# A float32 transpose: TensorE's start paced by a timed reading on VectorE

## The chip, the core and the metric

The kernel runs on one core of a Trainium2 chip. The metric is the device time of one execution in microseconds, median of three runs. Engines named below: TensorE (PE in the profile, its weight loads PEld), VectorE (DVE), ScalarE (ACT), GpSimd (POOL), SyncE (SP), and the DMA engines that move data between the chip's main memory and SBUF, the on-chip memory.

## The reference

The input x is an array of 8192 x 8192 float32 numbers, 268.4 MB; the output is its transpose:

```python
def reference(x):
    return np.transpose(x)
```

Nothing is computed but the new order. Every byte is read once from main memory and written once.

## The kernel before

**Tiling.** x is cut into T = 128 chunks of 128 rows and 4096 columns (2 MB each): 64 chunks down the left half of the columns, then 64 down the right half. A chunk is loaded by one DMA into `arena` (line 206), each partition holding one row of it. TensorE turns it by 32 transposes of 128 x 128 (line 368) into PSUM, in 16 groups g of two. Group g belongs to lane g of 16: 256 columns of x, which are 256 rows of the output.

**Storing along a diagonal.** Output rows are written in long stretches, so the groups of one lane from 16 successive chunks are collected and stored together, one lane per chunk: store w takes lane w modulo 16. Groups that are not yet due go from PSUM to `slots`; the one that is due in this chunk goes directly to its place in `arena` (line 297 does both). Just before, VectorE's "gather" (line 259) copies the 15 older groups of that lane from `slots` to their place in `arena`. ScalarE copies the first eight groups out of PSUM (half 0), VectorE the last eight (half 1). So the direct copy of chunk t is ScalarE's where t modulo 16 is 0 to 7, and VectorE's where it is 8 to 15. PSUM is full with one chunk: each half is freed for the next chunk when its engine's copies are done (line 305, semaphores s_fra and s_frv). TensorE signals after groups 4, 8, 12 and 16 (semaphore s_pe). Before a chunk's copies, both engines wait for the gather (line 272), since they overwrite what it reads.

**Stores and their space.** A store (line 28) of a full lane is 2 MB in one or two DMAs. The part of `arena` for stores has room for two and a fraction, so the gather for store u waits until store u - 2 has landed (line 247). Loads rotate over three places; the load of chunk t + 3 into the place of chunk t waits until the transposes of t are done. The first chunks are loaded further ahead, and the first and last 15 stores are shorter; the last ones ("flush") follow the last chunk.

**Order.** SyncE issues all loads and stores in one written order on one queue: store t - 1, load t + 2, store t, load t + 3 and so on. The other engines follow semaphores in the order of their own programs.

**TensorE's start.** For chunks E <= t < LAST (12 to 125) TensorE runs a loop over three chunks. Per chunk, in `transposes`: it waits until half 0 is free (line 358), runs IDLE = 4 products of the identity with four copies of itself, 128 x 512, into half 0 of PSUM (line 362, their result is overwritten), waits for the load (line 363), then for the semaphore s_go (line 365), and transposes; half 1 is waited for when group 8 is reached (line 358 again). A product is recorded as two matmuls in the profile. s_go is given by VectorE in `work`: it waits until store u - 2 has landed (line 398) and adds one (line 399), then makes the gather. Chunks before 12 and the last two have neither products nor s_go.

## Time and profile before

| What | Value |
|---|---|
| Median of three runs | 1273.62 us (1271.66 to 1286.72) |
| Profiled execution | 1275.6 us, span 1273.8 us |
| Moved | 537 MB, 422 GB/s on average |
| TensorE, matmuls | 959.7 us busy (75%) |
| TensorE, weight loads | 686.8 us (54%) |
| VectorE | 615.1 us (48%) |
| ScalarE | 257.4 us (20%) |
| Mean granted TensorE clock | 0.961 of full speed |

The span runs from the first to the last instruction of the profiled execution. Busy times include matmuls whose ends are modelled. In rows of the timeline the first number is the start in microseconds, the second the length from the first start to the last end of the merged instructions; in brackets stands how long the engine was idle before, and what released it. In rows of groups the numbers after the bar are the busy time in microseconds and the mean of one in nanoseconds, then the idle time before them. In rows of waits stand the total in microseconds, how many, and the longest. `L368` is line 368; PEq is TensorE's sequencer, whose line tells which wait held it.

### The profile page before, as it was taken

What the parts mean: (1) busy time and instruction counts of PE and PEld (TensorE: products, weight loads), DVE (VectorE), ACT (ScalarE), POOL (GpSimd) and SP (SyncE); (2) the same over time, 40 slices, a digit from 0 to 9 for tenths busy, and PEclk for the clock granted to TensorE, in tenths of its full rate; (3) what the DMA queues carried; (4) which work ended last, traced back from release to release, by engine and by line L of the source; (5) the groups of instructions that cost most, each with busy time, mean ns of one, the idle gap of its engine ahead of it and who ended that gap; (6) DMA issues with size and microseconds to landing.
All of it is one profiled execution on the core that took longest, in us unless ns stands there. A gap on an engine that the chain in (4) does not pass through costs nothing. (4 is left out here: it accounts for less than half of the span.)

```text
span 1273.8 us, 12854 instructions
## 1 busy us (share of the span) xinstructions
PE 959.7 (75%) x5008; PEld 686.8 (54%) x5008; DVE 615.1 (48%) x715; ACT 257.4 (20%) x402; POOL 0.7 (0%) x6
## 2 busy tenths in 40 slices
PE   6669787878777777778778777888877878878730
PEld 6656555555555555555555555655555655555530
DVE  3455455455445544545455444544544445444471
ACT  2222122112211211121112111122111221112210
POOL 0000000000000000000000000000000000000000
PEclk9879999999999999999999999999999899999965
DMA  9999999999999999999999999999999999999997
GB/s 393 411 422 417 427 432 429 431 432 428 432 431 432 432 428 433 431 431 432 428 428 429 431 430 429 424 402 428 396 431 430 422 419 418 425 430 428 417 397 323
DMA packets 41333, 537.09 MB, mean 422 GB/s; under 512 B 4576, under 2 KB 5216, under 8 KB 8288
## 3 DMA queue, kind: packets, MB, share of 16 engines
q1 hardware_dynamic: 41312, 536.89, 99.7%
q14 instruction: 17, 0.14, 0.0%
q8 instruction: 4, 0.07, 0.0%
HBM read 268.44 MB, written 268.44 MB: 421 GB/s over the span
## 5 line engine op out<-in xcount | busy, mean ns | idle before, releaser
L368 PE MATMUL ps<-ident,arena 128*128 128x128 f32 x4096 | 543.4, 293 | 206.2 <-PEq L365 166.8
L368 PEld LDWEIGHTS ps<-ident,arena 128*128 128x128 f32 x4096 | 523.4, 210 | 298.1 <-issue 298.1
L259 DVE COPY arena<-slots 128x2048 f32<-128x2048 f32 (+7 forms) x316 | 304.2, 1012 | 469.8 <-DMA out_dram<-arena 461.5
L362 PE MATMUL ps<-ident 128*128 128x512 f32 x912 | 418.0, 601 | 61.1 <-PEq L358 61.1
L297 ACT COPY slots<-ps 128x1024 f32<-128x1024 f32 (+2 forms) x335 | 238.4, 780 | 488.3 <-DVE arena L259 481.5
L297 DVE COPY slots<-ps 128x512 f32<-128x512 f32 (+2 forms) x336 | 289.4, 913 | 79.6 <-PE ps L368 79.6
L362 PEld LDWEIGHTS ps<-ident 128*128 128x128 f32 x912 | 164.0, 190 | 241.8 <-issue 241.8
L297 ACT COPY arena<-ps 128x256 f32<-128x256 f32 x66 | 24.5, 373 | 478.5 <-DVE arena L259 442.6
L297 DVE COPY arena<-ps 128x256 f32<-128x256 f32 x63 | 26.8, 425 | 87.1 <-PE ps L368 87.0
L297 ACT ACT_TABLE_LOAD x1 | 1.3, 1283 | 1.0 <-SPq L155 1.0
L341 POOL TENSOR_SCALAR_AFFINE_SELECT ident<-ident 128x128 f32<-128x128 f32 x1 | 0.3, 294 | 0.2 <-POOL ident L339 0.2
L339 POOL MEMSET ident<- 128x128 f32 x1 | 0.2, 206 | 0.5 <-SPq L155 0.5
L433 POOL MEMSET const-bfloat16-1.0<- 128x1 bf16 x1 | 0.1, 102 | 0.0
L433 POOL MEMSET const-uint8-127<- 128x1 uint8 x1 | 0.1, 102 | 0.0
L433 POOL MEMSET const-float32-0.0<- 128x1 f32 x1 | 0.1, 99 | 0.2 <-issue 0.2
L433 POOL MEMSET const-float32-1.0<- 128x1 f32 x1 | 0.1, 99 | 0.0
## 6 DMA issues: line engine op xcount, KB each, us to landing
arena<-in_x_dram SPq DMA_DIRECT2D x128, 2048.0 KB, 20.0
out_dram<-arena SPq DMA_DIRECT2D x98, 2048.0 KB, 16.3
out_dram<-arena SPq DMA_DIRECT2D x4, 1920.0 KB, 12.4
out_dram<-arena SPq DMA_DIRECT2D x4, 1792.0 KB, 11.5
out_dram<-arena SPq DMA_DIRECT2D x4, 1664.0 KB, 9.9
out_dram<-arena SPq DMA_DIRECT2D x4, 1536.0 KB, 10.2
out_dram<-arena SPq DMA_DIRECT2D x4, 1408.0 KB, 10.4
out_dram<-arena SPq DMA_DIRECT2D x4, 1280.0 KB, 11.8
```

The source lines that it names most:

```text
L259: cp = nc.vector.tensor_copy(out=ap(arena, do, [[P, len(v)], [dist, B], [1, P]]), in_=ap(slots, so, [[gap, len(v)], [P, B], [1, P]]),)
L297: cp = eng.copy(out=dst, in_=i) if e == 0 else eng.tensor_copy(out=dst, in_=i)
L339: nc.gpsimd.memset(ident, 0.0).then_inc(s_id, 1)
L341: nc.gpsimd.affine_select(out=ident, in_=ident, compare_op=mybir.AluOpType.not_equal, fill=1.0, base=0, pattern=[[-1, P]], channel_multipl ...
L362: nc.tensor.matmul(out=pss[0][:, :4 * P], lhsT=ident, rhs=four, start=True, stop=True)
L368: tr = nc.tensor.transpose(pss[h][:, (u * B + b) * P:(u * B + b + 1) * P], arena[:, q + b:q + PIECE - B + b + 1:B], ident,)
L433: nc = _bacc.Bacc("TRN2", target_bir_lowering=False, num_devices=1)
```

## The change

TensorE starts a chunk's transposes on another signal. VectorE no longer waits for store u - 2 ahead of s_go; it waits for the load of chunk u, takes the maximum over 27 readings of the identity (27 x 128 elements per partition; the result goes to `pad` and is not used), and gives s_go when that is done. The gather follows, with its own waits as before. TensorE now waits for both halves of PSUM at the start of a chunk, runs two products in place of four behind these waits, and waits for s_go ahead of the load's semaphore. All this holds for chunks 6 to 125 in place of 12 to 125.

```diff
-    E = 12
+    E = 6
...
-        nc.alloc_sbuf_tensor("pad", [P, 64], dt)
+        pad = nc.alloc_sbuf_tensor("pad", [P, 64], dt).ap()
...
+        REST = 27
...
-        IDLE = 4
+        IDLE = 2
...
-                if u == 0:
+                if u == 0 and not (h and E <= t < LAST):
                     nc.tensor.sem_inc(s_free[h], -1).wait_op(s_free[h], 1, "sem-ge")
                 if g == 0:
                     if E <= t < LAST:
+                        nc.tensor.sem_inc(s_free[1], -1).wait_op(s_free[1], 1, "sem-ge")
                         for _ in range(IDLE):
                             nc.tensor.matmul(out=pss[0][:, :4 * P], lhsT=ident, rhs=four, start=True, stop=True)
-                    nc.tensor.sem_inc(s_ld[o], -16).wait_op(s_ld[o], 16, "sem-ge")
                     if E <= t < LAST:
                         nc.tensor.sem_inc(s_go, -1).wait_op(s_go, 1, "sem-ge")
+                    nc.tensor.sem_inc(s_ld[o], -16).wait_op(s_ld[o], 16, "sem-ge")
...
                 if E <= u < LAST:
-                    free(nc.vector, ("S", u - 2))
-                    nc.vector.sem_inc(s_go, 1)
+                    nc.vector.wait_ge(s_ld[home["L", u]], 16)
+                    nc.vector.reduce_max(
+                        out=pad[:, :1], in_=ap(ident, 0, [[0, REST], [1, P]]), axis=mybir.AxisListType.XY
+                    ).then_inc(s_go, 1)
                 gather(u, u)
```

## The prediction

> **What bounds the kernel now.** I read the page first, then the waits, then one chunk in order of time.

> ```profile
> span 1273.8 us, 12854 instructions
> q1 hardware_dynamic: 41312, 536.89, 99.7%
> arena<-in_x_dram SPq DMA_DIRECT2D x128, 2048.0 KB, 20.0
> out_dram<-arena SPq DMA_DIRECT2D x98, 2048.0 KB, 16.3
> ```

> The transfers' one queue is busy 99.7% of the span: the DMA engines set the time. A transfer of 2 MB lands 16 to 20 us after its issue, although 2 MB at the 427 GB/s seen below last 4.9 us, so about 10 us of transfers are always queued. An engine may be late by some microseconds without emptying the queue.

> ```profile
> ACT slots L297 <- DVE arena L259: 481.5, 62, 13.6
> DVE arena L259 <- DMA out_dram<-arena: 461.5, 116, 11.4
> ```

> The waits agree: VectorE waits 461.5 us for stores, ScalarE then for VectorE's gather. The timeline shows chunk 65, and what starts chunk 66:

> ```profile
> 607.97 4.08 PE L368 MATMUL ps<-ident,arena 128*128 128x128 f32 x32 [1.48 <-PEq L365]
> 608.02 2.30 DVE L259 COPY arena<-slots 128x2048 f32<-128x2048 f32 x3 [4.17 <-DMA out_dram<-arena]
> ...
> 610.62 1.78 ACT L297 COPY slots<-ps 128x256 f32<-128x256 f32 x3
> ...
> 611.20 2.42 DVE L297 COPY slots<-ps 128x512 f32<-128x512 f32 x3 [0.89 <-PE ps L368]
> ...
> 612.59 3.67 PE L362 MATMUL ps<-ident 128*128 128x512 f32 x8 [0.54 <-PEq L358]
> ...
> 617.80 4.08 PE L368 MATMUL ps<-ident,arena 128*128 128x128 f32 x32 [1.54 <-PEq L365]
> 617.85 2.42 DVE L259 COPY arena<-slots 128x2048 f32<-128x2048 f32 x3 [4.23 <-DMA out_dram<-arena]
> ```

> Call P the start of a chunk's transposes (607.97) and "loop" the time to the next P (9.83 us here). VectorE is done with the copies at 613.62, P + 5.65, then idles 4.23 us until the store of two chunks ago lands. That slack of some four microseconds per chunk is what the change spends.

> ```profile
> 41.45:1204.77 1163.32, 916.92 (x4720) 645.35 (x4721) 564.68 (x655) 237.76 (x370) 0.00 (x0) 0.98 1.01 426
> ...
> 1204.77:1273.80 69.03, 14.57 (x96) 14.06 (x96) 32.75 (x38) 6.13 (x10) 0.00 (x0) 0.63 0.87 362
> ```

> Columns: PE, PEld, DVE, ACT, POOL busy, clock, DMA share, GB/s. Chunk 6 starts its transposes at 41.59, chunk 125 at 1204.77 (rows below): 119 loops of 9.775 us on average, at full DMA share.

> **The change, part by part.**

> The reading. VectorE now reads 27 x 128 = 3456 elements per partition before each gather. No row shows a reduction; the nearest are its copies:

> ```profile
> L297 DVE COPY slots<-ps 128x1024 f32<-128x1024 f32 x145 | 175.1, 1218 | 44.5 <-PE ps L368 44.5
> ...
> L297 DVE COPY slots<-ps 128x512 f32<-128x512 f32 x96 | 62.9, 683 | 28.3 <-PE ps L368 28.3
> ...
> L259 DVE COPY arena<-slots 128x2048 f32<-128x2048 f32 x126 | 153.5, 1219 | 244.5 <-DMA out_dram<-arena 243.2 <-issue 1.3
> ...
> L259 DVE COPY arena<-slots 128x1024 f32<-128x1024 f32 x20 | 13.6, 684 | 4.8 <-DMA out_dram<-arena 4.2 <-DVE slots L297 0.6
> ```

> Out of PSUM, 512 more elements cost 535 ns: 1.045 ns each and 0.148 us fixed. From SBUF to SBUF a copy goes at half that, 0.522 ns and 0.15 us. So 3456 elements take 3.75 us or 1.95 us. [...] I take 3.75 and keep 1.95 as an end. [...]

> What is behind the reading. VectorE's order is now: finish the copies, wait for the load, read, gather, copy. Everything that ScalarE (481.5 us of waits), SyncE's stores, and through the transposes the next load wait for, is queued behind it. VectorE's wait for the store two back is not removed: the gather itself makes it. What goes is TensorE's share of that wait. A chunk's load stands in the queue right ahead of the store two back, 4.9 us of transfer: that store landed by 617.8, so the load by 612.9, before the copies end (613.62). So the reading starts when VectorE is free.

> The loop. Two short hand-offs:

> ```profile
> 1209.30 2.14 DVE L297 COPY slots<-ps 128x1024 f32<-128x1024 f32 x3
> ...
> 1211.68 2.35 DVE L259 COPY arena<-slots 128x1792 f32<-128x1792 f32 x2 [0.24 <-DVE slots L297]
> ```

> From VectorE's last copy to its next operation is 0.24 us with the gather's two checks; the reading has one less, 0.15 taken. From a finished copy to TensorE is 612.59 - (610.62 + 1.78) = 0.19, say 0.2. Loop: 5.65 + 0.15 + 3.75 + 0.2 = **9.75 us**. In chunks whose number modulo 16 is 12 to 15, VectorE's first copy needs the last transposes:

> ```profile
> 875.95 4.07 PE L368 MATMUL ps<-ident,arena 128*128 128x128 f32 x32 [1.48 <-PEq L365]
> ...
> 880.13 0.42 DVE L297 COPY arena<-ps 128x256 f32<-128x256 f32 x1 [1.79 <-PE ps L368]
> 880.47 2.08 DVE L297 COPY slots<-ps 128x1024 f32<-128x1024 f32 x2
> ```

> The copies end at 882.55, P + 6.60, or with a fourth copy at 1209.30 + 2.14 - 1204.77 = P + 6.67; the loop is 10.72. Of the 119 loops from chunk 6 to 125, 29 are of this kind: 90 x 9.75 + 29 x 10.72 = 1188 us, mean 9.99, above the 9.775 of before. So the chain through VectorE, not the DMA, becomes the bound. The queue then drains, so stores and loads land earlier than now, and their waits are covered: a store lands 16.3 us after issue today and has some 17.

> E = 6. The chain starts at chunk 6:

> ```profile
> 41.45 0.96 DVE L259 COPY arena<-slots 128x1536 f32<-128x1536 f32 x1 [0.24 <-DVE slots L297]
> 41.59 5.49 PE L368 MATMUL ps<-ident,arena 128*128 128x128 f32 x32 [1.95 <-PEq L363]
> ...
> 1204.77 4.07 PE L368 MATMUL ps<-ident,arena 128*128 128x128 f32 x32 [1.69 <-PEq L365]
> ```

> With the reading at 41.45, P of chunk 6 is 41.45 + 3.75 + 0.2 = 45.4. After P of chunk 125, the table of stretches shows 362 x 69.03 = 25.0 MB still to move, and 69 us because the slowest transfers trail; with the queue drained before, about 25.0 MB / 427 = 58.5 us.

> Fewer products, later. Two products take 1.88 us (row below) and begin 0.2 after VectorE's copies, not ScalarE's. TensorE's time itself is free: it ends at P + 7.75 and the reading at P + 9.55. The cost is the clock. TensorE is idle from P + 4.08 to 5.85 (1.77 us) and from 7.75 to 9.75 (**2.0 us**); now the second gap is 1.54.

> ```profile
> 802.73:806.15 3.42, 1.52 (x6) 0.64 (x5) 0.37 (x1) 0.00 (x0) 0.00 (x0) 1.00 1.02 436
> 806.15:809.56 3.41, 3.41 (x18) 3.41 (x17) 2.06 (x3) 0.32 (x2) 0.00 (x0) 0.50 0.97 413
> ...
> 884.65:888.07 3.42, 1.24 (x10) 1.27 (x11) 1.19 (x2) 0.00 (x0) 0.00 (x0) 1.00 0.97 405
> 888.07:891.48 3.41, 3.41 (x18) 3.41 (x18) 1.16 (x2) 1.99 (x3) 0.00 (x0) 0.50 1.03 442
> ...
> 1024.60:1028.01 3.41, 1.63 (x13) 1.66 (x14) 1.59 (x2) 0.00 (x0) 0.00 (x0) 1.00 1.05 452
> 1028.01:1031.43 3.42, 2.89 (x22) 2.55 (x21) 2.59 (x4) 1.99 (x3) 0.00 (x0) 1.00 0.97 412
> ```

> ```profile
> 29.80 5.54 PE L368 MATMUL ps<-ident,arena 128*128 128x128 f32 x32 [2.27 <-PEq L363]
> ...
> 154.44 1.88 PE L362 MATMUL ps<-ident 128*128 128x512 f32 x4
> 158.55 4.08 PE L368 MATMUL ps<-ident,arena 128*128 128x128 f32 x32 [2.23 <-PEq L365]
> ...
> 985.83 5.55 PE L368 MATMUL ps<-ident,arena 128*128 128x128 f32 x32 [1.79 <-PEq L365]
> ...
> 1026.38 4.08 PE L368 MATMUL ps<-ident,arena 128*128 128x128 f32 x32 [2.10 <-PEq L365]
> ```

> In stretches of 3.41 us, at fixed places, TensorE busy for 1.52 or 1.24 us was followed by a stretch at half clock; busy for 1.63, it was not. The limit is about 1.6 us busy, 1.8 idle. Of the 12 gaps of 1.79 to 2.27 us ahead of transposes, eight were followed by slow ones (the first and last are shown, with two of the four exceptions). Slow transposes take 5.55 in place of 4.08; the copies end about 1.35 later, since one copy partly hides it. A stretch holds 1.8 us of a 2.0 us gap for (3.41 - 2.0 + 0.4)/3.41 = 53% of its positions; but the two kinds alternate: a warm loop, 9.75, is 0.49 short of three stretches and drifts toward the bad place, a cold one, 11.1, jumps 0.86 away, which balances at 0.49/1.35 = 36%. I take a third: 40 loops x 1.35 = 54 us.

> Sum: 45.4 + 1188 + 54 + 58.5 = 1346 us of span. The profiled execution took 1275.6 for its span of 1273.8, 1.8 more; it lies 0.2% above the median of the three runs (1273.62), so nothing is scaled. **Forecast 1348 us.**

> **The rivals.**

> *The clock stays whole.* Then the 54 us go: 1294 us. For it: four of twelve such gaps did no harm, the 1.8 limit is close to 2.0, and hand-offs 0.1 us shorter in two places would pass under it. [...]

> *The DMA stays the bound* (the other side). If the reading takes 1.95 us, the loop is 7.95, below 9.775; stores and loads then pace the chunks as now. It decides from 9.99 - 9.775 = 0.21 us per loop: a reading, with its hand-offs, shorter by that much hides. The time is that of before, less a few microseconds for steadier early chunks: 1270, within 1257 to 1282. For it: the SBUF source, and that 0.21 is little. Against: 3.60 us is what 3456 elements take at the single pace with no fixed cost.

> *Half clock in nearly every chunk.* If products also run slow, or the gap reaches 2.5 us, all 119 loops pay 1.35: 1294 + 161 = 1455. Against: slow transposes lengthen the busy time and move the next gap away.

> **How the numbers follow.** Forecast 0.50 (1318 to 1372, the slow share between a fifth and a half, the reading 3.60 to 3.85); whole clock 0.22 (1282 to 1310); DMA 0.21; half clock throughout 0.07. Two per cent, 1299 and 1248 us, is about what a measurement of this kernel tells from no change. Slower: 0.50 + 0.07 + 0.4 of 0.22 = 0.66; faster: 0.02, the DMA rival's tail; within 2%: 0.32. The range 1266 to 1372 leaves out a little under half of the DMA rival and the last one.

> **What would show it.** After: a reduction row x120 at 3.75 us; loops of 9.75 and 10.72 with some at 11; VectorE's idle time before the gather gone, transposes waiting for the line of the new semaphore; a PEclk line with 7s to 9s; DMA share under 1 and a mean below 410 GB/s; loads landing sooner than 20 us. The prediction is wrong if the reduction is near 2 us, if DMA share stays at 9s and GB/s near 422, or if the transposes' mean stays at 4.08 us per chunk.

## The result and the profile after

The changed kernel takes 1367.07 us (median of four runs, 1364.95 to 1369.63) against 1274.19 us for the kernel before: a ratio of 1.0709 (95% interval 1.0636 to 1.0781), 93 us more. The forecast was 1348 us within 1266 to 1372. In two experiments at the end, some executions were disturbed; ratios leave those out, so they lie below what the medians would give.

The page of the changed kernel, in the same parts as before:

```profile
span 1366.2 us, 12006 instructions
...
PEclk9989899889999789989999989999999988999985
DMA  9998999999999999999999999999999999999989
GB/s 394 402 341 336 393 428 408 400 363 399 406 391 413 363 387 408 403 399 369 394 405 415 406 383 396 403 398 407 384 390 426 403 402 359 406 394 396 406 362 386
...
L402 DVE TENSOR_REDUCE pad<-ident 128x1 f32<-128x3456 f32 x120 | 450.4, 3753 | 18.3 <-DVE slots L299 1.0
...
arena<-in_x_dram SPq DMA_DIRECT2D x128, 2048.0 KB, 12.0
out_dram<-arena SPq DMA_DIRECT2D x98, 2048.0 KB, 7.9
```

A reading takes 3753 ns, so 450 us of VectorE's time are new. The transfer rate has fallen by some 30 GB/s almost everywhere (393 GB/s on average, 422 before), and a load now lands 12.0 us after its issue (20.0 before), a full store 7.9 us (16.3). The queue is shallower than before: the engines come late with their issues, as the waits below confirm. The DMA row alone would hide this; it still shows nines.

Who waits for whom, in the changed kernel (total, times, longest):

```profile
PE ps L365 <- PEq L363: 241.6, 120, 3.1
...
PE ps L371 <- PEq L368: 210.7, 126, 8.5
...
DVE arena L261 <- DMA out_dram<-arena: 2.0, 1, 2.0
...
DVE pad L402 <- DMA arena<-in_x_dram: 0.4, 1, 0.4
```

VectorE waited 461.5 us for stores before; now 2.0 us for stores and 0.4 us for loads. No engine in the chain waits for a transfer any more. TensorE waits twice per chunk: for VectorE's copies before the products (L363), and ahead of the transposes. The second row names L368, the load's semaphore, because that is the last of two waits in a row; what is waited for is s_go on L367, given at the end of the reading. VectorE has waited for the same load before it reads, and in all 120 chunks the transposes start 0.30 to 0.34 us after the end of the reading.

The timeline of the changed kernel, from chunk 60 to 66 (starts and lengths in us):

```profile
614.40 4.07 PE L371 MATMUL ps<-ident,arena 128*128 128x128 f32 x32 [2.04 <-PEq L368]
...
618.93 2.08 DVE L299 COPY slots<-ps 128x1024 f32<-128x1024 f32 x2
...
621.15 3.75 DVE L402 TENSOR_REDUCE pad<-ident 128x1 f32<-128x3456 f32 x1
621.21 1.96 PE L365 MATMUL ps<-ident 128*128 128x512 f32 x4 [2.73 <-PEq L363]
...
625.20 4.08 PE L371 MATMUL ps<-ident,arena 128*128 128x128 f32 x32 [2.04 <-PEq L368]
...
636.42 5.55 PE L371 MATMUL ps<-ident,arena 128*128 128x128 f32 x32 [2.04 <-PEq L368]
...
642.42 2.14 DVE L299 COPY slots<-ps 128x1024 f32<-128x1024 f32 x3
...
644.71 3.75 DVE L402 TENSOR_REDUCE pad<-ident 128x1 f32<-128x3456 f32 x1
644.76 3.37 PE L365 MATMUL ps<-ident 128*128 128x512 f32 x4 [2.79 <-PEq L363]
...
648.76 4.07 PE L371 MATMUL ps<-ident,arena 128*128 128x128 f32 x32 [0.62 <-PEq L368]
```

```profile
659.55 4.08 PE L371 MATMUL ps<-ident,arena 128*128 128x128 f32 x32 [2.04 <-PEq L368]
...
662.78 2.42 DVE L299 COPY slots<-ps 128x512 f32<-128x512 f32 x3 [1.25 <-PE ps L371]
...
665.34 3.75 DVE L402 TENSOR_REDUCE pad<-ident 128x1 f32<-128x3456 f32 x1
...
669.39 1.80 PE L371 MATMUL ps<-ident,arena 128*128 128x128 f32 x13 [2.03 <-PEq L368]
```

Chunk 60 (60 modulo 16 is 12): transposes at 614.40, copies done at 621.01 (P + 6.61), reading from 621.15 to 624.90, next transposes at 625.20: a loop of 10.80. Chunk 64 (0 modulo 16): copies done at 665.20 (P + 5.65), next transposes at 669.39: a loop of 9.84. Chunk 62 has the same gap of 2.04 us in front and yet runs slow, 5.55 in place of 4.08: its loop is 12.34. There the granted clock was 0.50 from 637.39 to 640.80 us and again from 644.21 to 647.62; so the slowed clock reaches the next two products too (3.37 for 1.96), which shortens the gap after them to 0.62, and chunk 63 is whole again.

The stretches up to and behind the start of chunk 125's transposes (PE, PEld, DVE, ACT, POOL busy, clock, DMA share, GB/s):

```profile
45.25:1301.52 1256.27, 822.43 (x4284) 612.84 (x4285) 1000.20 (x775) 240.20 (x370) 0.00 (x0) 0.90 0.98 394
1301.52:1366.20 64.68, 13.71 (x96) 13.20 (x96) 32.37 (x38) 6.04 (x10) 0.00 (x0) 0.64 0.90 373
```

119 loops took 1256.3 us, 10.56 on average; before it was 9.775.

### The profile page after: what moved, and what is told of

Same layout as the page of the kernel before. It is cut to its first block, busy times and chain, and to the rows that moved or that the text cites. A ratio compares the mean times of both kernels' runs of the same rounds, so it can differ in the third digit from the quotient of the medians.

```text
span 1366.2 us, 12006 instructions
## 1 busy us (share of the span) xinstructions
PE 865.6 (63%) x4576; PEld 653.4 (48%) x4576; DVE 1054.2 (77%) x835; ACT 259.7 (19%) x402; POOL 0.7 (0%) x6
## 3 DMA queue, kind: packets, MB, share of 16 engines
q1 hardware_dynamic: 41312, 536.89, 97.3%
## 5 line engine op out<-in xcount | busy, mean ns | idle before, releaser
L371 PEld LDWEIGHTS ps<-ident,arena 128*128 128x128 f32 x4096 | 561.1, 212 | 332.1 <-issue 332.1
L371 PE MATMUL ps<-ident,arena 128*128 128x128 f32 x4096 | 581.6, 307 | 211.5 <-PEq L368 210.7
L402 DVE TENSOR_REDUCE pad<-ident 128x1 f32<-128x3456 f32 x120 | 450.4, 3753 | 18.3 <-DVE slots L299 1.0
L365 PE MATMUL ps<-ident 128*128 128x512 f32 x480 | 284.0, 722 | 241.6 <-PEq L363 241.6
L365 PEld LDWEIGHTS ps<-ident 128*128 128x128 f32 x480 | 92.4, 213 | 333.0 <-issue 333.0
## 6 DMA issues: line engine op xcount, KB each, us to landing
arena<-in_x_dram SPq DMA_DIRECT2D x128, 2048.0 KB, 12.0
out_dram<-arena SPq DMA_DIRECT2D x98, 2048.0 KB, 7.9
```

The costliest lines, as they stand in the source:

```text
L365: nc.tensor.matmul(out=pss[0][:, :4 * P], lhsT=ident, rhs=four, start=True, stop=True)
L371: tr = nc.tensor.transpose(pss[h][:, (u * B + b) * P:(u * B + b + 1) * P], arena[:, q + b:q + PIECE - B + b + 1:B], ident,)
L402: nc.vector.reduce_max(out=pad[:, :1], in_=ap(ident, 0, [[0, REST], [1, P]]), axis=mybir.AxisListType.XY).then_inc(s_go, 1)
```

## The experiments

Two theories were set against each other. The **chain theory** is that of the prediction: VectorE's copies, the reading and the hand-offs follow one another, and the slowed clock adds to some loops (the clock theory, where this part alone is meant). The **transfer theory** is the rival that the falling GB/s suggest: the readings of SBUF, or the new place of the work, disturb the transfers, which still set the time.

**Three products.**

```diff
-        IDLE = 2
+        IDLE = 3
```

> The change with three products in place of two. Chain theory (VectorE's copies, reading and hand-offs set the loop, 9.84 us or 10.81 us, and a half clock adds 1.5 us to a third of the chunks): the gap before the transposes shrinks from 2.04 to about 1.1 us, so no chunk of the kind 0 to 11 runs slow; the kind 12 to 15 still has 2.75 us before its products and may lose some 0.5 us each. 45 + 1200 + 10 + 65 = 1320 us. Transfer theory (the reading disturbs the transfers, which set the time at 393 GB/s): no product touches a transfer, so it stays at 1367 us.

Measured: 1317.99 us, ratio 1.034 (1.0302 to 1.0377), 49 us less than the change for one product more. TensorE in this kernel, from chunk 62 on:

```profile
632.83 4.51 PE L365 MATMUL ps<-ident 128*128 128x512 f32 x6 [2.73 <-PEq L363]
637.17 3.99 PE L371 MATMUL ps<-ident,arena 128*128 128x128 f32 x32
642.93 2.81 PE L365 MATMUL ps<-ident 128*128 128x512 f32 x6 [1.77 <-PEq L363]
646.92 4.08 PE L371 MATMUL ps<-ident,arena 128*128 128x128 f32 x32 [1.18 <-PEq L368]
```

With gaps of 1.77 and 1.18 us the transposes take 4.08 and the loop stays at 9.8. In the timeline the transposes of all 119 loops (kind 0 to 11 and kind 12 to 15, by the chunk's number modulo 16) take less than 4.4 us. Where 2.73 us lie ahead of the products, these take 4.51 for 2.81 and outlast the reading: it ended at 636.52, and the transposes start 0.65 us later in place of 0.30. So the idle stretch and the slowed clock behind it are worth 49 us of the 93. The transfer theory has no place for a product and can't be the whole of the loss; the readings from PSUM, below, test the rest.

**Four products.**

```diff
-        IDLE = 2
+        IDLE = 4
```

> The change with four products. With three, the chunks of the kind 12 to 15 were seen with 2.7 to 3.1 us of idle TensorE before the products, which then ran at half clock (4.5 to 5.5 us for 2.8) and ended only when the transposes should have begun. Clock theory: a fourth product adds 0.9 to 1.7 us at half clock to those 29 loops, partly at full clock again, some 0.6 us each, and nothing to the other 90, where four products end at P + 9.5 of 9.84: 1318 + 17 = 1335 us, slower than with three. If products only keep the clock up: no more than 1318 us.

Measured: 1342.39 us, ratio 1.0523 (1.047 to 1.0577): slower than three by 24 us, as the sign of the expectation has it (1335 forecast). TensorE in this kernel:

```profile
633.69 6.73 PE L365 MATMUL ps<-ident 128*128 128x512 f32 x8 [2.80 <-PEq L363]
640.25 3.99 PE L371 MATMUL ps<-ident,arena 128*128 128x128 f32 x32
```

Behind the copies of the kind 12 to 15, four products at half clock mostly take 5.1 to 5.4 us, here 6.73 (3.67 in the kernel before, in the row at 612.59), and outlast the reading by far, so TensorE itself delays the transposes. The loops of kind 12 to 15 average 11.59 us, against 11.01 with three products; those of kind 0 to 11 9.93 against 9.86.

**Readings from PSUM.**

```diff
-                        out=pad[:, :1], in_=ap(ident, 0, [[0, REST], [1, P]]), axis=mybir.AxisListType.XY
+                        out=pad[:, :1], in_=ap(pss[1], 0, [[0, REST], [1, P]]), axis=mybir.AxisListType.XY
```

> The change, but the 27 readings take half 1 of PSUM (128 columns of it, 27 times) in place of the identity in SBUF: as many elements, at the same pace. Chain theory: reading 3.75 us, loops of 9.84 and 10.81 us, a third of the chunks slow: 1367 us, within 1%. Transfer theory: without the readings of SBUF the transfers are no longer disturbed and the loss of 93 us goes, wholly or by the reading's part: 1275 to 1320 us.

Measured: 1370.55 us, ratio 1.0771 (1.0739 to 1.0803). Its group of readings:

```profile
L402 DVE TENSOR_REDUCE pad<-ps 128x1 f32<-128x3456 f32 x120 | 450.9, 3758 | 18.5 <-DVE slots L299 1.0 <-DMA arena<-in_x_dram 0.6
```

The same duration, the same total, and no reading of SBUF: the loss does not come from what the readings read.

**24 readings.**

```diff
-        REST = 27
+        REST = 24
```

> The change with 24 readings in place of 27: 3.36 us for 3.75. Chain theory: loops of 9.44 and 10.41 us, mean 9.68, below the 9.775 us of before, and the gap before the transposes falls to 1.65 us, under the 1.8 us at which the clock halves; so the DMA is the bound again, about 1270 us, with stores and loads landing 16 and 20 us after issue. Transfer theory: a ninth less reading takes off a ninth of the loss of 93 us: about 1357 us.

Measured: 1287.8 us, ratio 1.0101 (1.0059 to 1.0143). Three readings less give 79 us, far more than a ninth of the loss. The mean of the 119 loops falls from 10.56 to 9.86 us: 0.39 us is the shorter reading itself, and the rest is about what 26 fewer loops with slow transposes save (13 in place of 39). The expectation that a gap under 1.8 us would leave none did not hold. The chain and the transfers are now nearly even: loads and stores land 18.8 and 15.4 us after issue, and VectorE waits for stores again, though far less than the 461.5 us of before:

```profile
DVE arena L261 <- DMA out_dram<-arena: 36.2, 40, 2.1
```

But 1270 was forecast. The first two rows are of the kernel before, the last two of this one:

```profile
45.00:140.00 95.00, 69.75 (x401) 55.87 (x400) 46.71 (x56) 21.83 (x32) 0.00 (x0) 0.91 1.01 420
140.00:700.00 560.00, 443.37 (x2297) 306.83 (x2297) 274.67 (x319) 115.10 (x183) 0.00 (x0) 1.00 1.01 430
```

```profile
45.00:140.00 95.00, 65.25 (x337) 49.08 (x338) 67.52 (x56) 18.74 (x27) 0.00 (x0) 0.87 0.95 363
140.00:700.00 560.00, 366.83 (x2065) 274.04 (x2064) 460.29 (x370) 114.81 (x183) 0.00 (x0) 0.95 1.00 424
```

From 140 us on the transfers run at nearly the old rate. Between 45 and 140 us, 57 GB/s less over 95 us are 5.4 MB, some 13 us at the 427 GB/s of the kernel before from 119.02 to 1204.77 us, which is the whole difference in this profile. In the early chunks the stores are short, and in the kernel before the five loops from chunk 12 to 17 took 43.1 us, 8.6 each; the paced chain, with its mean loop of 9.86, does not let them.

**From chunk 12 on.**

```diff
-    E = 6
+    E = 12
```

> The change, but from chunk 12 on as before; 27 readings and two products stay. Chain theory: chunk 12 then starts at 95.1 us as in the kernel before, in place of 105.8, and every loop from there is that of the change: 1367 - 10.7 = 1356 us. Transfer theory: 114 readings in place of 120 take off a twentieth of the loss of 93 us: about 1362 us.

Measured: 1353.77 us, ratio 1.0636 (1.0598 to 1.0674), 13 us less than the change. The six earlier paced chunks cost about what the later start of chunk 12 says, in this kernel (10.7 us were forecast).

**Both.** 24 readings, and 20 readings, from chunk 12 on:

> 24 readings, from chunk 12 on. With 24 readings from chunk 6 on, chunk 17 started at 160.0 us, 21.9 us later than in the kernel before, with the transfers at 363 GB/s from 45 to 140 us; afterwards it caught up until the transfers set the loop again. Chain theory with this early loss: most of the 13 us between the two kernels goes, 1273 us, within 1270 to 1282. If the loss lies in the steady part, 6 loops of 120 change little: about 1286 us.

> 20 readings, from chunk 12 on: 2.82 us, loops of 8.9 and 9.9 us where the transfers allow, a gap of about 1.1 us before the transposes. Chain theory: the transfers are the bound throughout, 1270 us, within 1262 to 1278; a reading that hides costs nothing. Transfer theory: 20 of 27 parts of the loss of 93 us stay: about 1343 us.

Measured: a ratio of 1.0116 (1.0057 to 1.0176) with 24 readings, which is 1289 us beside the 1274 us of before, and of 1.0053 (1.0003 to 1.0102) with 20, which is 1281 us. The medians over all executions, 1293.49 and 1297.59 us, are higher; these spread from 1278 to 1304 and from 1275 to 1324 us, more than those of the kernel before (1270 to 1276). The transfer theory's 1343 is excluded, but 1273 and 1270 were not reached either. So leaving out the early pacing does not add to the shorter reading as I had summed it. Part of the reason stands in the traces, though those with 24 and 20 readings are of the longest of four executions each: with the short early stores, the five loops from chunk 12 to 17 take 43.1 us in the kernel before, but 55.5 us where the pacing begins at chunk 12 with 27 readings, 51.2 us with 24 and 50.4 us with 20. So 7 to 8 us are lost there though chunks 6 to 11 are not paced. What else the kernel with 24 readings loses, and why both are less steady, is open.

**The kernel before, with two products.**

```diff
-        IDLE = 4
+        IDLE = 2
```

> The kernel before with two products in place of four and nothing else. TensorE is then idle for some 3.3 us before most transposes. Chain theory: nearly every chunk runs at half clock, but VectorE has some 4 us of slack per chunk behind the store, so the time stays within 1% of 1274 us with transposes of 5.5 us. If a slow chunk costs its 1.4 us wherever it stands: 114 x 1.4 = 160 us more, about 1430 us.

Measured: 1271.79 us, ratio 0.9975 (0.9957 to 0.9993). In its timeline:

```profile
619.86 6.45 PE L368 MATMUL ps<-ident,arena 128*128 128x128 f32 x32 [3.66 <-PEq L365]
...
625.34 2.42 DVE L297 COPY slots<-ps 128x768 f32<-128x768 f32 x3 [3.01 <-PE ps L368]
...
629.80 2.43 DVE L259 COPY arena<-slots 128x2048 f32<-128x2048 f32 x3 [2.04 <-DMA out_dram<-arena]
```

Nearly every chunk was expected to be slowed; 79 of the 119 are, at a mean granted clock of 0.849. Here the transposes take 6.45 us, VectorE's copies end at 627.76 in place of some 625.5, and VectorE still waits 2.04 us for the store. The same slowed clock that cost 49 us in the changed kernel costs nothing here.

**The kernel before, without products.**

```diff
-        IDLE = 4
+        IDLE = 0
```

> The kernel before without products. Chain theory: transposes at half clock in nearly every chunk (5.5 us for 4.1), hidden in VectorE's slack of some 4 us behind the store: 1272 us, within 1% of before. If TensorE's clock is worth something where the transfers are the bound: 1.4 us in each of 114 chunks, less what two products already failed to save, so well above 1280 us.

Measured: 1271.43 us, ratio 0.9977 (0.9957 to 0.9997), with a mean granted clock of 0.755 and slow transposes in 114 of the 119 chunks. In the kernel before, the products buy nothing; leaving out some or all is even 3 us faster, the only versions here that beat it, by a quarter of a per cent.

**The kernel before, from chunk 6 on.**

```diff
-    E = 12
+    E = 6
```

> The kernel before with its loop from chunk 6 on and nothing else. Chain theory: chunks 6 to 11 start with the store of two chunks before, which their gather waits for anyway; no more than 5 us either way, 1270 to 1279 us. If the early start of the loop is what costs: chunk 12 started 10.8 us later after the change, so about 1285 us.

Measured: 1298.04 us, ratio 1.0152 (1.0111 to 1.0193). Neither 1274 nor 1285, and my reason was wrong:

```profile
40.15 3.67 PE L362 MATMUL ps<-ident 128*128 128x512 f32 x8 [0.42 <-PEq L358]
55.47 5.59 PE L368 MATMUL ps<-ident,arena 128*128 128x128 f32 x32 [11.65 <-PEq L365]
55.52 0.96 DVE L259 COPY arena<-slots 128x1536 f32<-128x1536 f32 x1 [14.23 <-DMA out_dram<-arena]
```

Chunk 6 waits 11.65 us for store 4. Its own gather does not need that store: the space of the first stores is still unused. The wait on a store two back is free from the chunk on at which the gather makes it anyway, and chunk 6 comes before that. This is only half of the loss in the profiled execution, though: chunk 12 starts 12.8 us later than in the kernel before, chunk 90 13.0 us, and chunk 125 27.7 us. What is lost behind chunk 90 is not explained.

## Why the prediction was right, and where it was off

| Term of the sum | Predicted, us | Measured, us |
|---|---|---|
| Start of chunk 6's transposes | 45.4 | 45.25 |
| 90 and 29 loops at whole clock | 1188 (9.75 and 10.72) | 1199 (9.84 and 10.80) |
| Half clock | 54 (40 loops x 1.35) | 57 (39 loops) |
| From chunk 125 to the end | 58.5 | 64.7 |
| Span | 1346 | 1366.2 |

- **The reading.** 3753 ns against 3.75 us: the pace of the copies out of PSUM with their fixed cost (1.045 ns an element and 0.148 us), though the source was SBUF; with PSUM as the source it was 3758 ns. No row of before has a reduction: that it goes at this pace, and not at the 0.522 ns of the copies from SBUF to SBUF, was the author's estimate.
- **The chain as the new bound.** Shown by the waits for transfers that fell from 461.5 to 2.4 us, by the landing times, and by the transposes that start 0.30 to 0.34 us after each of the 120 readings. The difference by position modulo 16, 0.97 us predicted, was 10.80 - 9.84 = 0.96.
- **The loop, 0.09 us short.** From the end of the reading (624.90) to the transposes (625.20) are 0.30 us, where 0.2 was taken from a place with one wait. TensorE now passes two there, the new semaphore and the load's. In the same kernel 0.20 us lie between the end of VectorE's copies (621.01) and the products (621.21), where the wait for half 0 is long over and one is left. That the second wait is the reason is argued only. Over 119 loops it makes the 11 us of the second row.
- **The clock.** The gap came out at 2.04 us (2.0 predicted), and 39 of 119 loops were slowed (25 of 90 and 14 of 29, counted in the timeline), against the third that was taken. Each cost 1.47 us, from (1256.3 - 1198.8)/39, not 1.35: that is the whole difference between 5.55 and 4.08, so the copy that was to hide part of it hid nothing. The third had been worked out from the gaps of the kind 0 to 11. Its rule, with three stretches of 3.413 us (from 802.73 to 1024.60 us of the kernel before there are 65 of them) and the measured loops of 9.84 and 11.31, gives (10.24 - 9.84)/(11.31 - 9.84) = 27% for that kind, and 25 of 90 are 28%. For the kind 12 to 15 the prediction overlooked that TensorE is idle for 2.73 us and more ahead of the products, not 1.77; there about half were slowed. That both together came to the 40 forecast is partly luck. Gaps of 2.04 us, as ahead of chunk 62, were enough here for half clock to follow.
- **The end.** 24.1 MB were left (373 x 64.68), near the 25.0 predicted, but they ran at 373 GB/s, not at 427. DMA share is 0.90 there: 10% of 64.7 us is about the 6 us missed. Most of it lies at the start, with shares of 0.82 and 0.76 (341 and 316 GB/s) in the first two stretches of 10 us. I had let the queue be full from the first moment; it had drained, as the sum itself said it would.
- **E = 6 as such.** Taken as part of the chain, and right for this kernel (13 us by experiment). The remark that the gather makes the store's wait anyway is wrong for the first chunks.
- **The rivals.** The whole clock is excluded by the 39 slow loops, the DMA bound by the waits, half clock throughout by the other 80.

## What to carry to other kernels

A delay that is cheap beside a long wait costs its full price as soon as the sum of the chain passes the period of what was waited for. Here 0.4 us per chunk, three readings in 27, were worth 79 us: 47 us in the loops themselves, and the rest through idle stretches that became short enough to keep TensorE's clock in more of the chunks (13 slow loops in place of 39). So price it as a loop (copies, delay, hand-offs, by kind of chunk), not as one more busy engine. Idle TensorE was harmless where its slow work ended inside another wait, and expensive where it stood in the chain: the half clock cost nothing in the kernel before (1271.43 us at a mean granted clock of 0.755) and 49 us after.
